# Contrast adjustment: the first tile leaves in three column pieces, and tiles 2 to 5 arrive in one transfer

One core of a Trainium2 chip runs the kernel. The metric is the device time of one execution in microseconds.

## The reference

```python
x = rand(16, 3, 512, 512) as float32; factor = 1.5
mean = np.mean(x, axis=(2, 3), keepdims=True)
return np.clip(mean + factor * (x - mean), 0, 1)
```

48 images of 1.05 MB: 50.33 MB in, 50.33 MB out.

## The kernel before

The data are cut into 12 tiles of [128 partitions x 8192 float32] (4.19 MB; a row of one partition is 32 KB). Each tile holds four whole images. A ring of six slots holds the tiles. A tile's mean needs the whole tile, so nothing of it can leave before all of it has come. Loads are issued by SP, stores by ACT, and the load of tile t+6 waits until tile t's store has landed. I number tiles from 0, as the program does.

```python
ROW = 8192; BUFS = 6; SHORT = 2048
FIRST = (SHORT, ROW - SHORT)
SUM = 4352
# ... (pools, weights for the mean)
def compute(t):
    # ... vector engine sums columns 0:SUM, scalar engine the rest; two matmuls make shift
    c = 0
    for n in FIRST if t == 0 else [ROW]:
        part = xt[:, c : c + n]
        nc.vector.tensor_scalar(part, part, factor, shift, mult, add)   # line 91 (shortened here)
        nc.vector.tensor_scalar(part, part, 0.0, 1.0, max, min)         # line 94
        store(t, c, c + n)
        c += n
# ...
load(0, c1=SHORT)
load(0, c0=SHORT)
load(1)
load(2, n=2)          # one transfer for tiles 2 and 3: both land together
load(4, n=2)
for t in range(n_tiles):
    compute(t)
    if t + BUFS < n_tiles:
        load(t + BUFS)
```

## Time and profile before

| | before |
|---|---|
| time, median (lowest to highest) | 239.27 us (239.07 to 239.33), 3 runs; 239.23 with 3 more |
| span of the profiled run | 237.3 us |
| bytes moved | 100.66 MB, mean 424 GB/s |
| vector engine busy | 163.1 us, 69% |
| tile 2's sum starts | 50.67 us |
| loads of tiles 6 and 7 issued (stores 0 and 1 landed) | 55.96, 76.55 us |

The prediction below shows the lines that most of these come from.

One caution for the GB/s row of such a page. Bytes are counted where a row's transfer ends. 442 GB/s x 5.93 us (a slice) is 2.62 MB, exactly 80 rows of 32 KB, five on each of the 16 DMA engines. So 442 is a count of whole rows. In the trace's packet records the median 32 KB row takes 1,213 ns on its engine, and 16 x 32,768 B / 1,213 ns = 432 GB/s is the steady rate. Slices of 403 to 436 between those of 442 are mostly slices in which a round of rows ends just outside: after 44 us no row of this trace takes over 1.3 us. Where I give bytes "moved by" a time below, I spread each row's bytes evenly over its time in those records.

### The profile page before, as it was taken

What the parts mean: (1) busy time and instruction counts of PE and PEld (TensorE: products, weight loads), DVE (VectorE), ACT (ScalarE), POOL (GpSimd) and SP (SyncE); (2) the same over time, 40 slices, a digit from 0 to 9 for tenths busy, and PEclk for the clock granted to TensorE, in tenths of its full rate; (3) what the DMA queues carried; (4) which work ended last, traced back from release to release, by engine and by line L of the source; (5) the groups of instructions that cost most, each with busy time, mean ns of one, the idle gap of its engine ahead of it and who ended that gap; (6) DMA issues with size and microseconds to landing.
All of it is one profiled execution on the core that took longest, in us unless ns stands there. A gap on an engine that the chain in (4) does not pass through costs nothing.

```text
span 237.3 us, 285 instructions
## 1 busy us (share of the span) xinstructions
PE 14.1 (6%) x48; PEld 12.0 (5%) x48; DVE 163.1 (69%) x38; ACT 43.2 (18%) x25; POOL 0.9 (0%) x9
## 2 busy tenths in 40 slices
PE   0010010001010001010010100100100100010000
PEld 0010010001010001010010100100100100010000
DVE  0079989048989328999989898891892795687000
ACT  2050230041050023050320504101400500500000
POOL 1000000000000000000000000000000000000000
DMA  7999999999999999999999999999999999999996
GB/s 297 410 442 442 421 442 359 456 439 441 442 436 414 403 431 442 442 442 442 436 442 436 414 409 425 442 442 442 442 436 442 436 420 403 425 442 442 442 442 265
DMA packets 3712, 100.66 MB, mean 424 GB/s; under 512 B 384, under 2 KB 384, under 8 KB 384
## 3 DMA queue, kind: packets, MB, share of 16 engines
q1 hardware_dynamic: 1840, 50.33, 49.7%
q10 hardware_dynamic: 1872, 50.33, 49.2%
HBM read 50.33 MB, written 50.33 MB: 424 GB/s over the span
## 4 chain that ended last, share of the span: by engine, by line
DMA 57%; DVE 29%; another core or an unknown queue 3%; PE 1%; SPq 1%; issue 0%; DVEq 0%
DMA ring<-in_x_dram 41%; DMA out_dram<-ring 16%; DVE sums L81 10%; DVE ring L91 9%; DVE ring L94 9%; PE bias L87 1%; SPq L76 1%; DVEq L91 0%
## 5 line engine op out<-in xcount | busy, mean ns | idle before, releaser
L81 DVE TENSOR_REDUCE sums<-ring 128x1 f32<-128x4352 f32 x12 | 56.2, 4683 | 45.7 <-DMA ring<-in_x_dram 45.7
L84 ACT ACTIVATE junk<-ring 128x3840 f32<-128x3840 f32 x12 | 40.8, 3403 | 163.3 <-DMA ring<-in_x_dram 107.5
L91 DVE TENSOR_SCALAR ring<-ring,bias 128x8192 f32<-128x8192 f32 (+2 forms) x13 | 54.1, 4163 | 8.9 <-PE bias L87 7.4
L94 DVE TENSOR_SCALAR ring<-ring 128x8192 f32<-128x8192 f32 (+2 forms) x13 | 53.3, 4099 | 0.4
L86 PE MATMUL bias<-sums,blockw 128*128 128x1 f32 x24 | 7.0, 361 | 190.8 <-ACT junk L84 190.8
L86 PEld LDWEIGHTS bias<-sums,blockw 128*128 128x128 f32 x24 | 6.0, 312 | 191.7 <-ACT junk L84 175.2
L87 PE MATMUL bias<-sums,blockw 128*128 128x1 f32 x24 | 7.0, 363 | 4.3 <-DVE sums L81 3.9
L87 PEld LDWEIGHTS bias<-sums,blockw 128*128 128x128 f32 x24 | 6.0, 311 | 5.3 <-DVE sums L81 5.0
L84 ACT ACTIVATION_READ_ACCUMULATOR junk<-ring 128x1 f32 x12 | 2.2, 186 | 0.0
L84 ACT ACT_TABLE_LOAD x1 | 1.3, 1283 | 0.7 <-PEq L129 0.7
L63 POOL MEMSET blockw<- 32x32 f32 x4 | 0.5, 117 | 0.2
L61 POOL MEMSET blockw<- 128x128 f32 x1 | 0.2, 204 | 0.3 <-POOLq L129 0.3
L129 POOL MEMSET const-bfloat16-1.0<- 128x1 bf16 x1 | 0.1, 111 | 0.0
L129 POOL MEMSET const-uint8-127<- 128x1 uint8 x1 | 0.1, 111 | 0.0
L129 POOL MEMSET const-float32-1.0<- 128x1 f32 x1 | 0.1, 108 | 0.0
L129 POOL MEMSET const-float32-0.0<- 128x1 f32 x1 | 0.1, 103 | 0.2 <-issue 0.2
## 6 DMA issues: line engine op xcount, KB each, us to landing
out_dram<-ring ACTq DMA_DIRECT2D x11, 4096.0 KB, 35.8
ring<-in_x_dram SPq DMA_DIRECT2D x7, 4096.0 KB, 49.7
ring<-in_x_dram SPq DMA_DIRECT2D x2, 8192.0 KB, 66.7
ring<-in_x_dram SPq DMA_DIRECT2D x1, 3072.0 KB, 11.7
out_dram<-ring ACTq DMA_DIRECT2D x1, 3072.0 KB, 28.2
ring<-in_x_dram SPq DMA_DIRECT2D x1, 1024.0 KB, 4.8
out_dram<-ring ACTq DMA_DIRECT2D x1, 1024.0 KB, 17.5
```

Of the source, the lines that this page charges most:

```text
L61: nc.gpsimd.memset(blockw, 0.0)
L63: nc.gpsimd.memset(blockw[a : a + ppi, a : a + ppi], wconst)
L76: nc.sync.dma_start(out=ring[:, b : b + n, c0:c1], in_=src)
L81: nc.vector.tensor_reduce(out=own[:, 0:1], in_=xt[:, 0:SUM], axis=mybir.AxisListType.X, op=Alu.add)
L84: nc.scalar.activation(out=junk, in_=xt[:, SUM:ROW], func=Act.Copy, accum_out=own[:, 1:2])
L86: nc.tensor.matmul(shift, blockw, own[:, 1:2], start=True, stop=False)
L87: nc.tensor.matmul(shift, blockw, own[:, 0:1], start=False, stop=True)
L91: nc.vector.tensor_scalar(out=part, in0=part, scalar1=factor, scalar2=shift, op0=Alu.mult, op1=Alu.add)
L94: nc.vector.tensor_scalar(out=part, in0=part, scalar1=0.0, scalar2=1.0, op0=Alu.max, op1=Alu.min)
L129: nc = _bacc.Bacc("TRN2", target_bir_lowering=False, num_devices=1)
```

## The change

The intent is to let the first tile's data leave earlier and in more even pieces, and to issue fewer, larger loads.

```diff
-FIRST = (SHORT, ROW - SHORT)
+FIRST = (SHORT, 3072, 3072)
@@
-        load(2, n=2)
-        load(4, n=2)
+        load(2, n=BUFS - 2)
```

## The prediction

> **What bounds the kernel now.** I read first the busy shares and the slices of the span, then the DMA queues, then the vector engine's groups by form, last the times at which transfers were issued.
>
> ```profile
> PE 14.1 (6%) x48; PEld 12.0 (5%) x48; DVE 163.1 (69%) x38; ACT 43.2 (18%) x25; POOL 0.9 (0%) x9
> DVE  0079989048989328999989898891892795687000
> DMA  7999999999999999999999999999999999999996
> GB/s 297 410 442 442 421 442 359 456 439 441 442 436 414 403 431 442 442 442 442 436 442 436 414 409 425 442 442 442 442 436 442 436 420 403 425 442 442 442 442 265
> DMA packets 3712, 100.66 MB, mean 424 GB/s; under 512 B 384, under 2 KB 384, under 8 KB 384
> ```
>
> The DMA row is the one that never falls: 90% or more in every slice but the first and last, at a plateau of 442 GB/s. 100.66 MB (input and output once each) at 442 GB/s are 227.7 us of the 237.3 us span. The other 9.6 us: some 2 us before data flows, 2.4 us in the last slice ((442-265)/442 of 5.93 us), the rest in shallow dips. The vector engine has 74 us idle. So the kernel ends early only if fewer bytes move (they don't) or the 16 DMA engines idle less; it ends late if both queues, loads on SP and stores on ACT, are ever empty together.
>
> The steady rate, dips included, I take from the load issues. A load waits for the store that frees its slot, so these are 19.3 to 19.5 us apart, in which one load and one store, 8.39 MB, move: **432 GB/s**.
>
> ```profile
> 95.98 0.33 SPq L76 DMA_DIRECT2D ring<-in_x_dram  x1
> 115.31 0.33 SPq L76 DMA_DIRECT2D ring<-in_x_dram  x1
> 134.71 0.33 SPq L76 DMA_DIRECT2D ring<-in_x_dram  x1
> 154.17 0.33 SPq L76 DMA_DIRECT2D ring<-in_x_dram  x1
> ```
>
> For a tile's compute:
>
> ```profile
> L81 DVE TENSOR_REDUCE sums<-ring 128x1 f32<-128x4352 f32 x12 | 56.2, 4683 | 45.7 <-DMA ring<-in_x_dram 45.7
> L91 DVE TENSOR_SCALAR ring<-ring,bias 128x8192 f32<-128x8192 f32 x11 | 49.4, 4491 | 8.2 <-PE bias L87 6.7 <-issue 1.5
> L94 DVE TENSOR_SCALAR ring<-ring 128x8192 f32<-128x8192 f32 x11 | 48.7, 4427 | 0.4
> L91 DVE TENSOR_SCALAR ring<-ring,bias 128x6144 f32<-128x6144 f32 x1 | 3.4, 3418 | 0.0
> L91 DVE TENSOR_SCALAR ring<-ring,bias 128x2048 f32<-128x2048 f32 x1 | 1.3, 1291 | 0.7 <-PE bias L87 0.7
> L94 DVE TENSOR_SCALAR ring<-ring 128x2048 f32<-128x2048 f32 x1 | 1.2, 1227 | 0.0
> ```
>
> 4.68 + 0.75 (wait for the mean) + 4.49 + 4.43 is 14.3 us, and where data is there the sums do follow each other by 14.28 us (116.19 to 130.47). The DMA needs 19.4 us for a tile's two transfers, so the vector engine catches up with any delay at 5 us per tile.
>
> The landings that the change touches:
>
> ```profile
> 50.67 4.69 DVE L81 TENSOR_REDUCE sums<-ring 128x1 f32<-128x4352 f32 x1 [8.77 <-DMA ring<-in_x_dram]
> 87.58 4.68 DVE L81 TENSOR_REDUCE sums<-ring 128x1 f32<-128x4352 f32 x1 [8.22 <-DMA ring<-in_x_dram]
> out_dram<-ring ACTq DMA_DIRECT2D x1, 3072.0 KB, 28.2
> out_dram<-ring ACTq DMA_DIRECT2D x1, 1024.0 KB, 17.5
> ```
>
> (I number tiles from 0, as the program does; the merged load brings tiles 2 to 5.) The pair 2, 3 is there at 50.67 us and the pair 4, 5 at 87.58. Tile 0's store pieces, issued at 20.91 and 27.64, landed at 38.4 and 55.8; tile 1's, issued at 41.94, let its load go at 76.55.
>
> **What the Trainium skill says.** "DMA: Bandwidth & Descriptors", section "Queues, rings and completion order", says that an engine with work on several queue rows takes them in turn, a packet at a time. The trace agrees if a packet is a row of a transfer: 3712 packets less 384 short ones (24 transfers x 16) are 3328 = 26 x 128 rows. Tile 0's second piece (24 KB rows) beside 32 KB load rows should get 24/56 of 432 GB/s = 185 GB/s: 3.15 MB in 17.0 us; it took 17.4 (38.4 to 55.8). "HBM Reference", "Specifications (TRN2)", gives about 358 GB/s per core, but about 425 for a core alone, bounded by its DMA engines; the mean here is 424. "VectorE: DVE Perf Modes", "The perf-mode tier table", lists fp32 tensor_scalar of 2048 elements at 1227 ns; the row above has 1227.
>
> **The change, part by part.**
>
> *Three pieces.* One 128x6144 pair becomes two of 128x3072. From 2048 to 6144 elements line 91 grows 0.519 ns per element, so 3072 take 1.82 us, line 94 about 1.76. Twice that is 7.17 us instead of 6.78; with the overlap of neighbours some 0.3 us more, during which the DMA is full of loads: free. The second piece is issued at 24.4 instead of 27.6 us, but it waits in the store queue behind the first (landed 38.4) in any case, so this gains nothing. What does change is the share: 12 KB rows get 12/44 of the turns' bytes, 118 GB/s, against 185. Tile 0's store then ends later: 3.15 MB / 0.118 = 26.8 us instead of 17, so at some 64 us of data and 65 us landed. The loads run faster meanwhile. 128 more rows are 8 per DMA engine; an estimate of 0.2 us at most.
>
> *One load for four tiles.* Two issues of 0.57 us become one of about 1 us. At the start it releases nothing early: tile 2 waits for all 16.8 MB. Its landing: by 37.4 us (the first piece's data end, about 1 us ahead of landing) (37.4 - 2.1) x 0.43 MB/us = 15.2 MB have moved, 1.05 of them stores, so 5.7 of the 16.8 MB are loaded. To 64.2 us loads get 32/44 of 0.43: 8.4 MB. The other 2.7 MB go half and half with tile 1's store: 12.4 us, to 76.6. **Tile 2 starts at about 77.6 us instead of 50.7**, tile 4 at 77.6 + 28.7 = 106.3 instead of 87.6. From there the vector engine never waits for data: tile 6's load is issued at 65 us, tile 7's at about 85.
>
> *Is the DMA ever empty?* Tile 2's store is issued at 77.6 + 14.4 = 92.0, tile 3's at 106.3, flowing some 2 us later, 108.3. Until then there is for the DMA: loads 0 to 7 and stores 0 to 2, 11 tiles of 4.19 MB = 46.1 MB, since load 8 waits for store 2 to land. At 0.43 they last 2.1 + 107.3 = **109.4 us**. So 1.1 us of margin. Earlier: by 94.0, when store 2 flows, loads 0 to 7 and two stores would last to 99.6; and between store 1's end (83.7) and load 7's first data (86.7) load 6 still has 2.7 MB, 6.2 us. After store 3 each period has 19.4 us of transfers against 14.3 of compute, so a backlog builds until load 11.
>
> *The end.* Back to back, tile 11's store is issued at 77.6 + 14.4 + 9 x 14.28 = 220.5 (218.2 before) and flows at 222.5. The DMA, full, would finish store 10 at about 235 - 9.7 = 225. So the vector chain has 2 to 3 us to spare, and the end stays the DMA's.
>
> *Sum.* Bytes, rate, start and tail as before: 239.27. Add 0.2 for shorter rows and 0.2 for the chance that the margin of 1.1 us is missed: **239.7 us**.
>
> **The rivals.**
>
> (a) *The late landing starves the DMA.* If stores got more of the turns than I think, say 24/56 as before, store 0 ends at 54.8, store 1 at 74, and the last 2.6 MB of the big load run alone, landing at 81.3. Then store 3 flows at 112 and the DMA is idle for 2.6 us: 241.9. Against it: the shares fit the trace. Past a landing of 78.7 each microsecond costs one. Losing 5 us, 2%, needs a landing near 83.5.
>
> (b) *It gains.* The 359 GB/s slice (35.6 to 41.5 us) lies where tile 0's first piece gives way to the second; more even pieces or a load without a seam might fill it. At most (442-359)/442 x 5.93 = 1.1 us: 238.2. But 456 follows it, so half of it is only counted late. The earlier store itself can't gain: the queue was never empty.
>
> (c) *A new semaphore wait.* The built program's order shows that the store of tile 7 now waits also for load 8, and the store of tile 5 for load 6. Load 8 should land near 131, tile 7 be ready at 163; load 6 near 91, tile 5 at 135. Both long past: no cost.
>
> **Range and chances.** Gain ends at (b), 238.2 to 238.5; loss by (a) is plausible to 2.5 us. 80% range 238.5 to 241.8. The 2% lines are at 234.5 and 244.1: faster 1%, within 95%, slower 4%.
>
> **What would show it.** Right: packets 3840; tile 2's sum starting at 77 to 79 us; the vector engine with one idle stretch of some 35 us before it and none for data after; the slices with DMA at 9 to the end; the chain now running from the big load straight through the vector engine's three lines. Wrong: a DMA digit under 9 in the slices from 100 to 115 us (then rival (a), worth its width), a lower plateau than 442 GB/s during the big load (then the merged rows are slower by themselves, which I priced at nothing), or vector idle time for data after 80 us.

## The result, and the profile after

| | before | after |
|---|---|---|
| time, median (lowest to highest, 6 runs each) | 239.23 us (239.07 to 239.40) | 239.86 us (239.57 to 240.71) |
| ratio | | 1.0034, 95% interval 1.0016 to 1.0052 |
| span of the profiled run | 237.3 us | 237.8 us |
| tile 2's sum starts | 50.67 us | 76.75 us (predicted 77.6) |
| tile 11's store ready | 218.2 us | 219.8 us (predicted 220.5) |

A ratio is the mean time of one kernel's fast runs over that of the other's of the same rounds, so it isn't quite the ratio of the medians.

The page of the changed kernel, its slices and its packets:

```profile
DVE  0079989100000899898999989899898999989000
DMA  7999999999999999999999999999999999999996
GB/s 280 426 441 441 423 441 421 396 442 433 415 462 424 435 402 419 441 441 430 435 441 424 441 435 441 424 413 435 435 435 430 441 435 435 441 430 435 413 430 265
DMA packets 3840, 100.66 MB, mean 423 GB/s; under 512 B 384, under 2 KB 384, under 8 KB 384
```

The vector engine now has one long hole (slices 8 to 12) and none after it. The DMA row is still 9 throughout: the hole cost the DMA nothing. In the packet records its engines stand idle for 0.01 us each between 5 and 235 us. 128 more packets are the 128 more rows.

The timeline, first the vector engine and then SP, of the changed kernel:

```profile
76.75 4.69 DVE L81 TENSOR_REDUCE sums<-ring 128x1 f32<-128x4352 f32 x1 [34.49 <-DMA ring<-in_x_dram]
105.36 4.68 DVE L81 TENSOR_REDUCE sums<-ring 128x1 f32<-128x4352 f32 x1
```

```profile
67.99 0.34 SPq L76 DMA_DIRECT2D ring<-in_x_dram  x1
87.42 0.33 SPq L76 DMA_DIRECT2D ring<-in_x_dram  x1
111.14 0.33 SPq L76 DMA_DIRECT2D ring<-in_x_dram  x1
```

Tile 4 starts at 105.36 us with no wait named; before, at 87.58 after a wait. The loads of tiles 6 and 7 were predicted at 65 and 85 us and came at 67.99 and 87.42. For tile 8's the prediction gives no time of issue; it came at 111.14, when tile 2's store had landed.

The waits (total us, times, longest) of the kernel before, and then of the changed one, say the same of the vector engine's idle time: about as much of it, in 2 waits instead of 7.

```profile
DVE sums L81 <- DMA ring<-in_x_dram: 45.7, 7, 13.0
```

```profile
DVE sums L81 <- DMA ring<-in_x_dram: 47.5, 2, 34.5
```

Where do the 0.4 to 0.6 us come from? By 50 us the changed kernel has moved 0.27 us' worth of bytes more than the kernel before; by 70 us it has lost that again, and from 100 us to the end it stays 0.2 us behind. The rest is at the very end. The bytes left in the last stretch, from 232 us on, of the kernel before and then of the changed one:

```profile
DMA packets 55, 1.28 MB, mean 242 GB/s; under 512 B 16, under 2 KB 16, under 8 KB 16
```

```profile
DMA packets 60, 1.44 MB, mean 249 GB/s; under 512 B 16, under 2 KB 16, under 8 KB 16
```

0.16 MB more are 0.37 us at 432 GB/s. The records carry no engine number. When I put the rows together into 16 chains by matching ends to starts, the chains of the kernel before end between 235.5 and 236.1 us, those of the changed one between 235.5 and 236.6: the engines are less in step, and the slowest sets the end.

### The profile page after: what moved, and what is told of

It is laid out like the page before. It is cut to its first block, busy times and chain, and to the rows that moved or that the text cites. A ratio compares the mean times of both kernels' runs of the same rounds, so it can differ in the third digit from the quotient of the medians.

```text
span 237.8 us, 286 instructions
## 1 busy us (share of the span) xinstructions
PE 14.0 (6%) x48; PEld 12.0 (5%) x48; DVE 162.9 (69%) x40; ACT 43.2 (18%) x25; POOL 0.9 (0%) x9
```

## The experiments

My theory (A in the expectations): the kernel ends when its bytes have moved at 432 GB/s; order, pieces and merging count only where both queues, loads and stores, are empty at once. The rivals: short rows cost time by themselves (R), a merged load costs time by itself (M), the vector engine has become the bound (V), earlier data gives an earlier end (E).

| run | loads of tiles 2 to 5 | rows of tile 0's store, KB | time, us | ratio (95%) |
|---|---|---|---|---|
| the change again | one | 8, 12, 12 | 239.55 | 1.0018 (1.0006 to 1.0030) |
| pieces_only | two | 8, 12, 12 | 239.60 | 1.0016 (1.0004 to 1.0028) |
| merged_only | one | 8, 24 | 243.15 | 1.0170 (1.0157 to 1.0183) |
| merged_8kb | one | 8, 8, 8, 8 | 239.76 | 1.0035 (1.0022 to 1.0048) |
| merged_noclip | one | 8, 24 | 239.52 | 1.0012 (0.9997 to 1.0026) |
| merged_split3 | one | 8, 24 | 241.03 | 1.0078 (1.0064 to 1.0093) |
| merged_five | one, with tile 1 | 8, 12, 12 | 248.86 | 1.0405 (1.0392 to 1.0419) |
| pairs_graded | two | 4, 8, 20 | 239.53 | 1.0007 (0.9994 to 1.0021) |
| pairs_8kb | two | 8, 8, 8, 8 | 240.72 | 1.0066 (1.0054 to 1.0079) |
| one_piece | two | 32 | 241.49 | 1.0101 (1.0086 to 1.0115) |
| singles | four | 8, 24 | 241.73 | 1.0101 (1.0074 to 1.0128) |
| pairs_4kb | two | 8 x 4 | 248.44 (244.39 to 253.08) | 1.0264 (1.0217 to 1.0310) |

Results were correct except where wrong on purpose.

### Each half of the change alone

`pieces_only` is the change's first hunk alone.

```diff
-FIRST = (SHORT, ROW - SHORT)
+FIRST = (SHORT, 3072, 3072)
```

> Only the three pieces; loads stay in pairs. Theory A (12 KB rows get 12/44 of the DMA's bytes; the DMA stays full; only the bytes count): store 0 lands near 68 us as in the changed kernel (tile 6's load is issued then, not at 56), the loads run ahead meanwhile, so tile 2's sum starts near 47 us instead of 50.7 and tile 4's near 77 instead of 87.6; the time is that of before plus 0 to 0.3 us: ratio 1.000 to 1.0015. Rival R (the +0.6 us of the change comes from the 128 extra short rows or the piece seams): ratio 1.002 to 1.004. Rival M (it comes from the merged load): ratio 1.000.

Measured 239.60 us, ratio 1.0016. Tile 2's sum starts at 47.69 us, tile 4's at 77.70: as expected. The ratio lies between the theory's and the rival's, and the interval covers both. The profiled run was the fastest of the five (239.31), and its bytes are 0.07 us behind those of before: it doesn't show the 0.4 us of the median.

`merged_only` is the second hunk alone.

```diff
-        load(2, n=2)
-        load(4, n=2)
+        load(2, n=BUFS - 2)
```

> Only the load of tiles 2 to 5 in one; tile 0 leaves in 8 and 24 KB rows. Theory A (what counts is whether tile 3's store is ready before 46.1 MB have moved, about 109.4 us): store 0 lands near 56, store 1 near 76, so the big load lands last, near 81 us; tile 3's store flows at 81 + 30.7 = 112, the DMA runs empty for 2 to 3 us somewhere between 105 and 115 us, and the time is 241 to 242.2: ratio 1.007 to 1.013. Rival R (short rows cost the 0.6 us): tile 0's rows are as before, ratio 1.000, no hole. Rival M (merging costs 0.6 us by itself, no hole): ratio 1.002 to 1.004.

Measured 243.15 us, +4.0: a hole, as expected, but dearer than the 2 to 3 us. Tile 2's sum starts at 81.54 us. The DMA and GB/s rows of its page (slices of 6.04 us, so whole rounds show as 434), the issue of tile 3's store, then three stretches with DMA share and GB/s in the last two columns:

```profile
DMA  7999999999999999997999999999999999999995
GB/s 296 432 434 429 396 433 403 456 422 463 434 429 434 434 423 434 429 434 288 385 429 358 434 434 434 434 434 434 434 434 434 434 434 434 434 434 434 434 434 217
```

```profile
110.25 0.34 ACTq L101 DMA_DIRECT2D out_dram<-ring  x1
```

```profile
100.00:108.00 8.00, 1.06 (x4) 0.89 (x4) 7.21 (x3) 0.00 (x0) 0.00 (x0) 1.00 1.01 434
108.00:116.00 8.00, 1.17 (x4) 1.00 (x4) 7.25 (x3) 3.50 (x2) 0.00 (x0) 1.00 0.93 328
116.00:124.00 8.00, 0.00 (x0) 0.00 (x0) 7.97 (x2) 0.00 (x0) 0.00 (x0) 1.00 0.89 385
```

Here is what the prediction's rival (a) described. Tile 3's store was issued at 110.25 us, after the 46.1 MB had run out at 109.6. Its first row flowed at 111.10, 0.85 us after the issue. The engines stood still for about 1.4 us each. The share in 108 to 116 us fell only to 0.93 while the rate fell to 328 GB/s, because rows are slow as well. The first two rounds of rows after the hole take their usual time, 1.23 to 1.25 us; the slow ones come at 113.6 and in the first rows of tile 8's load, at 115.3 to 115.9 (it was issued at 110.78), with up to 2.8 us instead of 1.2, and again at 128.6 to 131, where tile 3's store ends and tile 4's begins. Slow rows account for 2.1 us more per engine than in the kernel before, 1.3 and 0.7 at these two places. By 140 us the kernel is 3.5 us of transfers behind. So one half of the change loses 4.0 us, the other 0.4, and both together 0.3 to 0.6: the pieces repair the merge. They hold tile 0's store back, so the loads get more of the DMA and land 4.8 us earlier (76.75 against 81.54).

`after_again` is the changed kernel once more.

> The changed kernel once more, as a measure of how well its small loss repeats. If the loss is real: 239.6 to 240.2 us, ratio 1.002 to 1.005. If the first six runs were a chance: ratio within 0.001 of 1.

Measured 239.55 us, 1.0018 (1.0006 to 1.0030): just under what was expected of a real loss, and outside what was expected of chance. The loss repeats, since the interval leaves out 1; by the medians it is 0.3 us here and 0.6 in the first set.

### More room

`merged_8kb` moves the landing further away from the threshold.

```diff
-FIRST = (SHORT, 3072, 3072)
+FIRST = (SHORT,) * 4
```

(against the changed kernel)

> The load of tiles 2 to 5 in one, tile 0's store in four pieces of 8 KB rows. Theory A: stores get only 8/40 of the bytes, so the big load lands earlier than in the changed kernel, near 70 to 71 us (76.75 there), store 0 lands at about the same time, 71 to 74, and from there the margin to an empty DMA is about 8 us: time as before plus 0 to 0.4 us, ratio 1.000 to 1.002. Rival R: 256 extra rows against 128 in the change, so twice its loss: ratio 1.005 to 1.006. Rival M: as the change, 1.002 to 1.004.

Tile 2's sum starts at 70.21 us: the share of 8 KB rows holds. The time, 239.76 us, ratio 1.0035, is over what theory A gave (at most 1.002) and inside rival M's range. But its bytes are never over 0.03 us behind those of before from 70 us on; what it loses, it loses in the last rows. Six microseconds more of margin gain nothing, so the margin isn't what the change pays for. Rival R, at 1.005 or more, falls. A cost of merging of a few tenths of a us (M) is not excluded: this run can't tell it from any other loss in the last rows.

### Is it the hole?

`merged_noclip` gives a wrong result on purpose. Without the clip a tile needs 9.9 us of vector work.

```diff
-            nc.vector.tensor_scalar(
-                out=part, in0=part, scalar1=0.0, scalar2=1.0, op0=Alu.max, op1=Alu.min
-            )
```

(against merged_only)

> Wrong result on purpose: merged_only without the clip instruction, so 9.9 us of vector work per tile instead of 14.3. Theory A: the big load still lands near 81 us, but tile 3's store is issued near 101 us, flows at 103, ahead of 109.4 when the bytes run out: no hole, 239.3 to 240.2 us, ratio 1.001 to 1.005, with the vector engine waiting for data again later. Rival V (the late start makes the vector engine the bound; its chain sets the end): the time falls well below 239 us. Rival M: 242.5 to 243.5.

Measured 239.52 us, ratio 1.0012. Tile 2's sum starts at 81.46 us, as late as in merged_only, and 3.6 of the 4.0 us are gone. So neither the merged rows (M) nor the late landing by itself make the 4.0 us (a few tenths are within the interval). V falls too, by the trace of merged_only: tile 11's store was issued at 224.57 us, and its engines stand idle for only 0.02 us each from 116 to 235, so the DMA sets the end there. The test isn't clean, as less vector work moves every later store too; the next run moves one store alone. The same stretch as above, of merged_noclip:

```profile
108.00:116.00 8.00, 0.88 (x4) 0.79 (x4) 7.66 (x2) 3.50 (x2) 0.00 (x0) 1.00 1.03 442
```

`merged_split3` closes the hole with a right result: tile 3 leaves in two halves.

```diff
-        for n in FIRST if t == 0 else [ROW]:
+        for n in FIRST if t == 0 else [ROW // 2] * 2 if t == 3 else [ROW]:
```

(against merged_only)

> As merged_only (one load for tiles 2 to 5, tile 0 in 8 and 24 KB rows: +4.0 us), but tile 3 leaves in two halves, the first some 4.4 us earlier (issued near 105.9 instead of 110.25 us). Theory A (the loss is the hole at 109.6 to 111 us, in which both queues are empty until tile 3's store comes): the hole closes, 239.4 to 240.3 us, ratio 1.001 to 1.005, though the big load still lands near 81.5 us. Rival M (a big load that lands late costs by itself, say by rows that run 4 MB apart in one transfer): 242.5 to 243.5 as before.

Measured 241.03 us: half a miss. Its first half was issued at 105.91 us, and the hole is gone; but a new loss appears later. Stretches of merged_split3:

```profile
108.00:116.00 8.00, 1.17 (x4) 1.00 (x4) 7.22 (x4) 3.50 (x2) 0.00 (x0) 1.00 1.00 430
...
134.00:150.00 16.00, 1.17 (x4) 1.00 (x4) 15.20 (x5) 3.50 (x2) 0.00 (x0) 1.00 1.01 410
```

From 134 to 150 us the DMA is fully busy (1.01) at only 410 GB/s: the rows are slower. In the records they take 1.3 to 2.7 us at 134 to 136, where the load of tile 9 begins beside a store, and at 142 to 146 us, where one store gives way to the next. That costs 1.1 us. Such a seam my theory didn't have. So closing the hole wins back 2.1 of the 4.0 us by the medians. (The profiled run, 241.87, was the slowest of the six.)

### One tile further

```diff
-        load(1)
-        load(2, n=BUFS - 2)
+        load(1, n=BUFS - 1)
```

(against the changed kernel)

> One step further: tiles 1 to 5 in one load, tile 0 in the change's three pieces. Theory A: the big load lands near 71.4 us and is followed only by load 6, which ends near 80; tile 1's store flows at 71.4 + 14.4 + 2 = 87.8, so the DMA is empty for 7.7 us; it is empty for 3 us more near 97 to 100, after store 1, until load 7 flows. Sum 10.7 us, with slow first rows after each hole 1 or 2 more: 249 to 253 us, ratio 1.04 to 1.06, and the hole near 80 to 88 us is seen in the slices. Rival (the landing time alone matters, and 71.4 is under the 78.7 of my prediction): 239.5 to 241.

Measured 248.86 us, ratio 1.0405: 0.14 us under the expected range. Tile 1's sum starts at 71.39 us (71.4 expected). Its DMA and GB/s slices, and the stretch of the hole:

```profile
DMA  7999999999999098999999999999999999999996
GB/s 297 461 430 420 424 428 419 392 433 445 433 424 424 0 424 334 345 424 424 424 446 440 446 424 430 435 430 430 424 424 451 440 435 430 424 424 424 430 435 265
```

```profile
80.00:88.00 8.00, 0.00 (x0) 0.00 (x0) 7.97 (x3) 1.80 (x1) 0.00 (x0) 1.00 0.30 127
```

Two holes came, as expected, but narrower: 80.5 to 86.7 us and 96.4 to 98, in all 7.9 us per engine and not 10.7. Tile 1's store was issued at 85.81 and flowed at 86.66, tile 7's load at 96.99 and 97.95: under 1 us each, where I had put 2. Slow rows make the rest (1.5 us) of the 9.5 us that the trace is behind, as expected; the range was missed by the width of the holes.

A landing at 71 us is early by the threshold of 78.7 us, yet the DMA runs dry: what counts is how many bytes are queued behind the landing, and that is worked out anew for each order. Only one load was (4.19 MB, 9.7 us), against 14.4 us until tile 1's store.

### What the rest of the loss is

Four runs looked at rows and seams with the loads in pairs or single.

```diff
-FIRST = (SHORT, ROW - SHORT)
+FIRST = (1024,) * 8              # pairs_4kb
+FIRST = (SHORT,) * 4             # pairs_8kb
+FIRST = (ROW,)                   # one_piece
+FIRST = (1024, 2048, 5120)       # pairs_graded
```

(each alone, against the kernel before)

> Doubles and more the suspected cost of short rows: loads in pairs as before, tile 0's store in eight pieces of 4 KB rows, 768 extra rows (6 times the change's 128). Rival R: 6 x 0.5 us = 3 us or more, ratio 1.012 to 1.017. Theory A: stores get 4/36 of the bytes while loads run, so tile 0's slot comes free only when the first loads are through, near 70 us; the DMA is never empty; at most 0.5 us for rows and seams: ratio 1.000 to 1.003.

248.44 us as the median of all six runs; three count as slow (over 1.5% above the fastest; the clock reads 1.00 in all), the fast ones are 244.39, 244.46 and the profiled 247.54: a miss for both theories, and a faulty experiment. With more transfers the program's semaphores were dealt out otherwise, and the second pair's load had to wait until a piece of the store had landed; SP issued it at 46.54 us (at about 2.7 us before):

```profile
46.54 0.38 SPq L76 DMA_DIRECT2D ring<-in_x_dram  x1
```

Transfers fall behind by 1.0 us between 40 and 50 us. The larger part is at the end: two of the 16 chains of rows end 6 to 8 us after the others. What put just two engines so far behind stays open.

> Short rows once more, without the fault of pairs_4kb (there the second pair's load had to wait for a piece of the store to land; here its only wait is for a load that lands at 13 us). Pairs, tile 0 in four pieces of 8 KB rows: 256 extra rows. Theory A (rows cost 8 ns each beyond their bytes: 16 more per DMA engine, 0.13 us): 239.2 to 239.7 us, ratio 1.000 to 1.002. Rival R (short rows cost 0.5 us per 128): ratio 1.004 or more. If pairs_4kb's loss came from short rows at all, some of it should show here too: over 1.005.

240.72 us, ratio 1.0066: a miss for theory A, and by its number what rival R expected. But a row's own cost doesn't make it: merged_8kb has the same four pieces and takes 239.76. In the records an 8 KB row takes 309 ns, a 12 KB row 460, a 24 KB row 912 and a 32 KB row 1,213: about 8 ns beyond the bytes per row. 16 more rows per engine are 0.13 us, 8 more (the change) 0.06 us. In the trace of pairs_8kb 0.3 us of transfers are lost by 100 us; most of the rest is at the end, where the chains of rows end between 235.4 and 237.6 us. Why they do so here and not in merged_8kb (235.5 to 236.4) stays open.

> Pairs, tile 0 leaves whole: one seam in the store queue less than before (at the seam of tile 0's two pieces, 36 to 40 us, rows stretch and some 0.7 us of transfers are lost in the trace of before). Its store starts 6.4 us later, but loads fill the DMA until then. Theory A: an earlier store is worth nothing, 238.4 to 239.3 us, ratio 0.9965 to 1.0005. Rival E (the early first piece is worth its 6 us or part of it): 240 us or more.

241.49 us, ratio 1.0101: a miss. The earlier first piece is worth something. The stretch of the kernel before, and then of one_piece, whose only store of tile 0 was issued at 27.41 us, with rows of 32 KB:

```profile
28.00:36.00 8.00, 1.18 (x4) 1.00 (x4) 7.25 (x2) 3.50 (x2) 0.00 (x0) 1.00 0.96 414
```

```profile
28.00:36.00 8.00, 1.17 (x4) 1.00 (x4) 7.25 (x2) 3.39 (x2) 0.00 (x0) 1.00 0.99 356
```

0.99 busy at 356 GB/s: no hole, but slow rows, of up to 2.9 us. They are rows of the load that is under way, from 28.9 us on; the store's own first rows, at 32.2, take 1.21 us. By 40 us one_piece is 0.7 us behind, and never makes it good. So that part of the loss isn't the lateness of the store. The other 1 us of the trace is at the end (the last chain ends at 237.8 us, 236.1 before); what makes it isn't shown. Before, the same happens in smaller portions: at 24 to 28 us (first piece, 8 KB rows) and at 36 to 40 (24 KB rows begin). I had called the latter's 359 GB/s slice half a matter of counting. Slow rows of 1.4 to 1.8 us there are real: some 0.5 us (the 0.7 in the expectation was read off too coarse a stretch).

> Pairs, tile 0 in three pieces of 4, 8 and 20 KB rows. In the traces so far rows stretch for some 4 us where a store stream starts beside loads or steps up in row size: most in one_piece (32 KB rows from nothing, down to 302 GB/s at 30 us), less with 8 KB rows first (401 to 409). Theory S (the size of the step sets the loss): 4, 8, 20, 32 KB are smaller steps than 8, 24, 32, so no more than before: 238.7 to 239.4 us, ratio 0.998 to 1.001. Rival N (each seam costs, whatever its step): one seam more than before, 239.5 to 240.3, ratio 1.0015 to 1.005.

239.53 us, ratio 1.0007. The ratio is that of theory S (at most 1.001), the time a little over its 239.4, and the interval still holds part of N's range. By 40 us its transfers are 0.48 us ahead of before, by 70 us 0.06 behind: by this one trace smaller steps up to 20 KB save, and the step to 32 KB rows takes it back. It doesn't beat before.

`singles` loads each of the tiles 2 to 5 for itself.

```diff
-        load(2, n=2)
-        load(4, n=2)
+        for t in range(2, BUFS):
+            load(t)
```

> The opposite of merging: tiles 2 to 5 each with its own load, tile 0 in 8 and 24 KB rows. Tile 2's sum can start some 8 us earlier than with pairs, near 38 to 42 us. Theory A (all bytes flow anyway, the DMA is never empty): as before within 0.3 us, ratio 0.999 to 1.0015. Rival E (earlier data gives an earlier end): under 0.99.

241.73 us (240.45 to 242.67), ratio 1.0101: a miss. Tile 2's sum starts at 41.83 us, nine earlier than before, and the end is later, so here earlier data doesn't give an earlier end (E). Of the 2 us in its profiled span (239.3) 0.4 are transfers lost bit by bit; the remainder lies in chains of rows that end up to 2 us after the others, at 237.9 us. Why the engines drift apart here I can't say.

No version tried beats the kernel before.

## Why the prediction was right

The median was 239.86 us against 239.7 predicted, in a range of 238.5 to 241.8. By its own steps:

- **The bound.** Right: 432 GB/s from start to end. Wrong in reading 442 GB/s as a plateau with dips; 442 is a count of whole rows. The sum used 432, so nothing came of it.
- **The shares of the queue.** Right in direction, coarse in size. From 37.4 to 67 us the two 12 KB pieces moved 3.15 MB, 106 GB/s, where 12/44 of 432 gives 118. The records show what was left out: loads and stores do take turns row by row, but the 4-byte record that closes a piece takes a turn too, with a load row before and after it. A piece of 8 rows per engine then has 9 turns: 8 x 12 of 8 x 12 + 9 x 32 KB is 25%, 108 GB/s. So tile 6's load came 3 us later than predicted, and the big load 0.85 us earlier.
- **The vector engine's late start costs nothing.** Right. It starts tile 2 26 us later, runs without a wait for data from there, and as the DMA is never idle to the end, the vector engine doesn't set the end.
- **The margin before tile 3's store.** Right in outcome, and the step that mattered; its size was wrong. A store flowed 0.85 us after its issue (merged_only) and not 2, the landing was 0.85 us early, and the other 46.1 MB lasted to about 110 us instead of 109.4. By these figures I estimate a margin of some 3.5 us, where the prediction had 1.1, and a limit near 80.3 us for the landing instead of 78.7. With the landing at 76.75 us the DMA was never empty; with 81.54 (merged_only) it was. Rival (a) put that case at 81.3 us and 2.6 us of loss. The place is right, the size too small: 4.0 us. The hole itself was narrower, 1.4 us (again because of the 0.85), but slow rows after it cost 2.1 us more, which the prediction had nothing for.
- **No new semaphore wait.** Right: the stores of tiles 5 and 7 were issued at 134.07 and 162.65 us, 0.03 us after their last vector instruction, so neither waited for a load.
- **The extra 0.4 us.** The size is about right (0.6 and 0.3 us in the two sets), both named causes are not. Short rows cost 0.06 us, not 0.2, and the margin wasn't missed. What the traces show instead is 0.2 to 0.3 us of transfers lost at seams and 16 engines that end less in step. It was luck that these sum to what I put down for others.
- **The chain.** I expected the chain of waits to run from the big load through the vector engine. The view of the changed kernel reaches back only to 167 us and ends there in time for which it names no cause, so it neither shows nor refutes that.

What stays open: why rows stretch where a stream begins or changes its row size, and why the engines drift apart by different amounts. The experiments show that both happen and how much they cost, not what makes them. So what makes the change's last 0.3 to 0.6 us is not shown; that its late landing costs no more than this is.

## What to carry to other kernels

Where the DMA is busy from end to end, count bytes, not landings: a late landing is free as long as enough is queued behind it, and the microsecond at which the queued bytes run out can be worked out beforehand from the rate and the order of issues. Two halves of a change can depend on each other; here the split of one store makes room for a merged load that alone would cost 4 us. When what is left is under 1%, look at where transfer streams begin and at how far apart the DMA engines end, not at the busy share.

## What the Trainium skill lacked or had wrong

- "DMA: Bandwidth & Descriptors", "Queues, rings and completion order", counts typically 9 to 17 descriptors to a packet, which an engine drains before it changes queue. Here an engine changes queue after every row: put into chains by matching ends to starts, a row is followed by one of the other queue in 424 of 431 cases from 42 to 76 us of the changed kernel. The profile counts one packet for each row (3,328 and 3,456 long packets for 26 x 128 and 27 x 128 rows). So the row length sets a queue's share: 106 of 432 GB/s for 12 KB rows beside 32 KB rows. No page says that the record which closes a transfer costs its queue a turn; here it lowers the share from 12/44 (118 GB/s) to a quarter (108 GB/s; 106 measured).
- The same page's "Rules for kernel authors" advises coalescing small transfers. No page puts a figure on what merging large ones can cost, by their later landing, where the DMA is busy throughout. One load of 16.8 MB instead of two of 8.4 MB cost 4.0 us here by itself.
- No page says that rows get slow where a stream of transfers begins beside another: up to 2.9 us for a 32 KB row instead of 1.213, and 356 GB/s over 8 us in one_piece with the engines 0.99 busy. After a hole it isn't so in each case: the first rows of stores took 1.21 to 1.24 us (merged_only, merged_five), those of a load 1.4 to 2.2 (merged_five).
